# Stick-breaking and differential attention units alternate, and adaLN's rows run between their projections

## The chip, the cores and the metric

One Trainium2 chip; the kernel runs on one core. The metric is the device time of one execution in microseconds (us). The times of before are three runs; a profiled execution stands beside them.

## What is computed

One layer of a hybrid encoder on 1024 prompt rows and 64 sample rows of width 1024, with 1024 cached positions for the sample. All of it is float32; the kernel splits operands into a high and a low part and multiplies three times where it needs float32's precision.

```python
sh1, sc1, ga1, sh2, sc2, ga2 = split(silu(c) @ w_ada + b_ada)   # adaLN
u = (rmsnorm(x) * (1 + sc1) + sh1) @ w_in
# 4 differential heads of 2 x 64: softmax with ALiBi and a chunk mask
a = softmax(s_0) - lam * softmax(s_1);  od = rmsnorm(a @ vd) * (1 - 0.2)
# 8 stick-breaking heads of 64, strictly causal
between = reverse_cumsum(log_sigmoid(-z)) - log_sigmoid(-z)
osb = exp(log_sigmoid(z) + between) @ vs
x = x + ga1 * rmsnorm(concat(od, osb) @ w_out)
x = x + ga2 * rmsnorm(relu(h2 @ w_up)**2 @ w_down)              # h2 from x, sc2, sh2
```

Keys and values of both groups are outputs as well.

## The kernel before

The program has five stages: a setup that loads x and adaLN's first columns, eight attention **units**, the output projection (L1059 to L1062), the feed-forward in 16 blocks, and the end. This case is about the units. Units 0 to 3 are the differential heads, units 4 to 7 are pairs of stick-breaking heads; `unit_cols` (L308) gives the 128 columns of `w_in` that belong to a unit.

A unit consists of three kinds of work:

- **The projection** `proj(u, g)` (L545): q, k and v of the unit for three groups of rows, g = 0, 1, 2 with 384, 384 and 320 rows (`GRP`). Each (u, g) is 72 matmuls in `dense_T` (L303 to L305), 216 for a unit. VectorE (DVE) and ScalarE (ACT) read the result out. After g = 2 of a unit the next unit's weights are loaded and split.
- **Eight steps** over the queries. A differential step `Diff(u, t)` (L635) takes 128 queries: products `pz` (L575, L576), on DVE a minimum with the distance table (L660), on ACT `Exp` (L624), then on DVE the combination of the two softmaxes (L682), transposes on PE (L586), split by ACT and DVE (L64, L65), and the products with V (L602, L603). A stick-breaking step `Stick(u, q, hd)` (L722) takes 256 queries of one head: the products, on ACT two `Sigmoid` (L738, L739), a mask on GpSimd (L720), on DVE a scan along the keys (L712) and a product (L713), then transposes, splits and the products with V (L759, L760).
- **One `Sample(u)`** (L791): the 64 sample rows against the cache, with `Exp` for units 0 to 3 and `Sigmoid` (L867 and the line after it) and scans for units 4 to 7. It stands among the steps of a later unit.

The order is written out by hand. `sections` (L959 to L968) lists the steps unit by unit, 0 to 7, and inserts the samples. The main loop runs the application of one step together with the scores of the next (`merge`, L947) and spends from a `Filler` (L910) meanwhile: a list of projections and of adaLN's remaining rows. `need` (L970) says by which step a projection must be done: group 0 by a unit's first step, group 1 by its third, group 2 by its seventh. So groups 1 and 2 of a unit and group 0 of the next are done during a unit. A scheduler then places the instructions on each engine.

adaLN's **rows** (`rows`: four `gate_rows`, eight pieces of `modulation`; L201, L209, L245) are twelve pieces of filler work. Each loads two blocks of 512 KB of `w_ada` into the three `raw` buffers that the units' weights, the cache and the distance tables use too. Before, two pieces follow the projection's group 2 in each of units 2 to 5, one in unit 6 and three in unit 7 (`others`, L994).

The output projection waits for `mixD`, to which each unit writes its rows, and for their split into `mh` and `ml` (L64, L65).

Of the kernel before, what the change touches and what calls it, by code (L numbers as in the profile page):

```python
# [16 lines left out]
P = 128  # L17
D = 1024
KT = D // P
# [7 lines left out]
GRP = ((0, 384), (384, 384), (768, 320))  # L27
NTT = 9


# [4 lines left out]
def build(tc, I, O):  # L35
    nc = tc.nc
# [274 lines left out]
    def proj_weights(u, i):  # L311
        c = unit_cols(u)[i]
        return weights(w_in[:, :, c : c + P], [P, KT, P], f"w{'qkv'[i]}{u}", el=nc.vector if u == 0 else None)

# [42 lines left out]
    def first(k):  # L357

        for i in range(3):
            drain(dense_T(PS[i], PW[0, i], hT, 0, (k,)))  # L360

    few_columns()
    w0 = [big(f"w{i}0r", "raw", [P, KT, P], F32) for i in range(3)]
    for i in range(3):
        PW[0, i] = big(f"w{i}0h", "w", [P, KT, P]), big(f"w{i}0l", "w", [P, KT, P])

    def first_weights(half, up=False):
        ks = slice(4 * half, 4 * half + 4)
        for i in range(3):
            c = unit_cols(0)[i]  # L370
            if up:
                load(w0[i][:, ks], w_in[:, ks, c : c + P])
                continue
            split(w0[i][:, ks], *(t[:, ks] for t in PW[0, i]), el=nc.vector)

# [97 lines left out]
    def proj_q(u, g, wq):  # L473
# [4 lines left out]
        Q = U[u]["Q"]  # L478
        if u + g:
            ps = bank(f"pq{u}{g}", "pj")  # L480
            yield from dense_T(ps, wq, hT, g)
        else:
            ps = PS[0]
# [10 lines left out]
    def proj_k(u, g, wk):  # L494
# [4 lines left out]
        Kd, Kl = U[u]["Kd"], U[u]["Kl"]  # L499
        if u + g:  # L500
            ps = bank(f"pk{u}{g}", "pj")
            yield from dense_T(ps, wk, hT, g)
        else:
            ps = PS[1]
# [14 lines left out]
    def proj_v(u, g, wv):  # L519
# [3 lines left out]
        V = U[u]["V"]  # L523
        if u + g:
# [20 lines left out]
    def proj(u, g):  # L545
        for i, f in enumerate((proj_q, proj_k, proj_v)):
            if (u, i) not in PW:
                PW[u, i] = proj_weights(u, i)
            for n, c in enumerate(f(u, g, PW[u, i])):
                yield c  # L550

                if u == 0 and g == 1:
                    n += (0, 8, 17)[i]
                    if n >= 5 and (n - 5) % 2 == 0 and (n - 5) // 2 < KT:
                        k = (n - 5) // 2
                        block_mod(block_T(2, k, "tr"), 2, k, nc.gpsimd, k % 2 == 1)
                        yield 0.4
            if g == 2 and u < 7:
                PW[u + 1, i] = proj_weights(u + 1, i)

# [398 lines left out]
    sections = []  # L959
    for u in range(4):  # L960
        sections.append([Diff(u, t) for t in range(8)])
    for u in range(4, 8):
        sections.append([Stick(u, q, hd) for q in range(4) for hd in range(2)])
    for u in range(7):
        if u != 3:
            sections[u + 1].insert((1,1,2,2,1,1,2)[u], Sample(u))
    sections[3].append(Sample(3))
    sections[7].insert(8, Sample(7))  # L968
    steps = [st for sec in sections for st in sec]
    need = []  # L970
    for u in range(8):
        sec = [st for st in sections[u] if not isinstance(st, Sample)]
        for st, g in zip((sec[0], sec[2], sec[6]), range(3)):
            need.append((steps.index(st), (u, g)))
    need.append((len(steps) + 1, "end"))
    cost = [st.cost for st in steps]
    drain(proj(0, 0))
    ready_1()
# [14 lines left out]

    others = {2: (rows, 2, 2), 3: (rows, 2, 2), 4: (rows, 2, 2), 5: (rows, 2, 2), 6: (rows, 1, 1), 7: (rows, 3, 3)}  # L994
    for u in range(8):
        for g in range(3):
            if u + g:
                fill.add(proj(u, g), 12, (u, g))
            if g == (2) and u in others:
                gen, n, c = others[u]  # L1000
                fill.add(some(gen, n), c, "end" if u == 7 else None)
    steps[0].ready()
# [267 lines left out]
```

## Time and profile before

| | us |
|---|---|
| median of three runs | 1586.6 (1586.38 to 1587.48) |
| the profiled execution, its own time | 1589.58 |
| its span | 1587.9 |
| setup (span's start to unit 0) | 54 |
| units 0 to 7 (54 to 694) | 640 |
| output projection (694 to 807) | 113 |
| feed-forward and end (807 to 1588) | 781 |

A unit begins where PE starts its first product `pz`; the boundaries come from the program order of PE laid against the trace. Times in the trace count from the span's start. PE's busy time overlaps itself, since a matmul's end is modelled: how far apart two matmuls start is a better measure of what one costs. In windows of the trace the columns are: the stretch, its length, busy us of PE, PEld (weight load), DVE, ACT and POOL (GpSimd) with the number of instructions in brackets, PE's granted clock as a share of full speed, the share of the DMA engines and GB/s.

### The profile page before, as it was taken

The page shows a single profiled execution, that of the slowest core. Times are in us where ns is not written, and L with a number is a line of the kernel's source. Part 1 is how long each engine was busy: PE and PEld are TensorE (multiplying, and loading weights), DVE is VectorE, ACT ScalarE, POOL GpSimd, SP SyncE. Part 2 cuts the span into 40 slices and gives each one's busy share as a digit, 9 for nine tenths or more (in the row PEclk, how much of TensorE's full clock was granted, in tenths as well). Part 3 has the DMA queues.
Part 4 walks back from the last instruction along what each step waited for, and adds up shares of the span by engine and source line. Part 5 has one row for each costly group of instructions (what it writes and reads, how often), then busy time and mean ns, then how long its engine had stood idle before and what let it go on. Part 6 is the DMA issues. An engine that isn't in the chain of part 4 may idle for free.

```text
span 1587.9 us, 23684 instructions
## 1 busy us (share of the span) xinstructions
PE 1517.0 (96%) x8682; PEld 1357.9 (86%) x8682; DVE 987.2 (62%) x1880; ACT 703.3 (44%) x1665; POOL 366.7 (23%) x580
## 2 busy tenths in 40 slices
PE   6899999999999999789999999999999999999998
PEld 3689988988888889667889888999999899999896
DVE  3777676778789888995552455445544445544447
ACT  3867675766666667656563221121221121221132
POOL 0444352526353434451120000000000000000003
PEclk9999999998999999879999999999999999999999
DMA  9322142432322222364220222021111011111025
GB/s 309 115 60 87 55 116 84 135 95 76 95 74 85 69 70 78 103 208 161 97 63 27 80 80 78 17 79 53 54 42 52 28 41 53 54 41 53 27 80 179
DMA packets 152518, 133.22 MB, mean 84 GB/s; under 512 B 11233, under 2 KB 136274, under 8 KB 152402
## 3 DMA queue, kind: packets, MB, share of 16 engines
q1 hardware_dynamic: 152402, 131.71, 27.2%
q8 instruction: 68, 1.11, 0.3%
q14 instruction: 48, 0.39, 0.1%
HBM read 108.59 MB, written 23.09 MB: 83 GB/s over the span
## 4 chain that ended last, share of the span: by engine, by line
PE 74%; DVE 12%; issue 4%; ACT 3%; DMA 2%; POOL 1%; SPq 0%; POOLq 0%; DVEq 0%; ACTq 0%
PE pu L303 8%; PE pu L304 8%; PE pu L305 8%; PE pd L1145 8%; PE pd L1146 8%; PE pd L1148 7%; DVE k L712 4%; PE py L1059 2%; PE py L1060 2%; PE pt L586 2%; DVE s L713 2%; PE py L1062 2%; PE pq L304 1%; PE pq L303 1%; PE pq L305 1%
## 5 line engine op out<-in xcount | busy, mean ns | idle before, releaser
L1152 DVE TENSOR_TENSOR acc<-pd,acc 128x512 f32<-128x512 f32 x252 | 171.9, 687 | 113.3 <-PE pd L1148 107.2
L1130 ACT ACTIVATE sq<-pu 128x384 f32<-128x384 f32 (+1 forms) x96 | 45.2, 471 | 310.8 <-PE pu L305 310.8
L1131 DVE TENSOR_TENSOR sq<-sq 128x384 f32<-128x384 f32 (+1 forms) x96 | 72.1, 751 | 174.7 <-ACT sq L1130 174.7
L65 DVE TENSOR_TENSOR al<-pt,ah 128x512 fp32r<-128x512 f32 (+2 forms) x128 | 75.5, 599 | 25.7 <-ACT ah L64 24.9
L575 PE MATMUL pz<-K,Q 128*128 128x512 f32 (+2 forms) x192 | 74.8, 393 | 6.4 <-ACT k L739 2.2
L64 ACT CAST ah<-pt 128x512 fp32r<-128x512 f32 (+2 forms) x128 | 65.4, 523 | 33.6 <-PE pt L586 23.2
L586 PE MATMUL pt<-ident,s 128*128 128x128 f32 x432 | 73.7, 288 | 3.3 <-DVE s L713 2.6
L624 ACT ACTIVATE s<-s,mn 128x512 f32<-128x512 f32 (+3 forms) x96 | 58.5, 611 | 26.7 <-DVE mn L660 25.4
L576 PE MATMUL pz<-Kl,qz 128*128 128x512 f32 (+2 forms) x192 | 69.8, 369 | 0.0
L712 DVE TENSOR_TENSOR_SCAN k<-k 128x127 f32<-128x127 f32 (+3 forms) x64 | 62.1, 980 | 4.3 <-POOL k L720 4.0
L713 DVE TENSOR_TENSOR s<-s,k 128x383 f32<-128x383 f32 (+3 forms) x96 | 62.9, 662 | 1.4
L586 PEld LDWEIGHTS pt<-ident,s 128*128 128x128 f32 x432 | 53.1, 147 | 7.6 <-DVE s L713 3.3
L65 DVE TENSOR_TENSOR rl<-sq,rh 128x384 fp32r<-128x384 f32 x64 | 35.7, 558 | 37.9 <-ACT rh L64 37.9
L738 ACT ACTIVATE s<-pz 128x512 f32<-128x512 f32 (+2 forms) x96 | 48.1, 501 | 16.5 <-PE pz L576 12.0
L575 PEld LDWEIGHTS pz<-K,Q 128*128 128x128 f32 x192 | 38.3, 200 | 15.1 <-ACT k L739 4.5
L64 ACT CAST rh<-sq 128x384 fp32r<-128x384 f32 x64 | 32.9, 514 | 40.2 <-DVE sq L1131 38.2
L739 ACT ACTIVATE k<-pz 128x512 f32<-128x512 f32 (+2 forms) x96 | 48.4, 504 | 4.9 <-DVE k L712 4.0
L442 POOL CAST qz<-Q 64x256 fp32r<-64x256 f32 x64 | 34.7, 542 | 66.3 <-PE pz L576 63.9
L760 PE MATMUL po<-al,V 128*128 128x256 f32 (+1 forms) x160 | 43.5, 306 | 6.7 <-DVE al L65 6.6
L759 PE MATMUL po<-ah,V 128*128 128x256 f32 (+1 forms) x160 | 44.9, 292 | 0.5 <-ACT ah L64 0.5
L720 POOL TENSOR_SCALAR_AFFINE_SELECT s<-s 128x128 f32<-128x128 f32 x64 | 30.1, 470 | 63.6 <-ACT s L738 62.9
L660 DVE CUSTOM_DVE_ANT_0 s<-pz,T 128x512 f32<-128x512 f32 (+3 forms) x64 | 37.2, 585 | 10.8 <-PE pz L576 10.3
(1227 smaller groups left out, 5211.3 us busy)
## 6 DMA issues: line engine op xcount, KB each, us to landing
arr<-in_w_ada SPq DMA_DIRECT2D x16, 512.0 KB
arm<-in_w_ada SPq DMA_DIRECT2D x16, 512.0 KB
ar<-in_w_ada SPq DMA_DIRECT2D x10, 512.0 KB
mixD<-mx SPq DMA_DIRECT2D x32, 128.0 KB
xr<-in_x_prompt SPq DMA_DIRECT2D x16, 256.0 KB
xD<-xr SPq DMA_DIRECT2D x16, 256.0 KB
xy<-xD SPq DMA_DIRECT2D x8, 512.0 KB
out_y_prompt<-xy SPq DMA_DIRECT2D x16, 256.0 KB
```

Source lines behind the costliest of these rows:

```text
L64: (eh or nc.scalar.copy)(hi, src)
L65: (el or nc.vector).tensor_tensor(lo, src, fr(hi), ALU.subtract)
L303: mm(ps[:, :n], lhsT=wh[:, k, :], rhs=hh[:, k, :n], start=(k == 0), stop=False)
L304: mm(ps[:, :n], lhsT=wh[:, k, :], rhs=hl[:, k, :n], start=False, stop=False)
L305: mm(ps[:, :n], lhsT=wl[:, k, :], rhs=hh[:, k, :n], start=False, stop=(k == 7))
L575: mm(ps[:, :w], lhsT=S["Q"][m][:, qt], rhs=S["Kd"][m][:, c0 : c0 + w], start=True, stop=False)
L586: nc.tensor.transpose(pt[:kr, i * P : (i + 1) * P], a, ident)
L712: nc.vector.tensor_tensor_scan(k, k, k, 1.0 if c == n - 1 else kp[c + 1][:, 0:1], ALU.mult, ALU.bypass)
L1145: mm(ps, lhsT=rh[:, off : off + P], rhs=wh[:, cols], start=(j == 0), stop=False)
L1146: mm(ps, lhsT=rh[:, off : off + P], rhs=wl[:, cols], start=False, stop=(m == 8 and end))
L1148: mm(ps, lhsT=rl[:, off : off + P], rhs=wh[:, cols], start=False, stop=end)
L1152: nc.vector.tensor_tensor(acc[m][:, cols], ps, acc[m][:, cols], ALU.add)
```

## The change

The units run in the order 4, 0, 5, 1, 6, 2, 7, 3. The sample of each unit stands after the second step of the unit behind it, the last one's before its own last step. The twelve pieces of rows follow groups 0 and 1 of the projections of the third to the eighth unit in the order, one each. Everything that was bound to unit 0 as the first (the weights that the setup prepares, the projection that it finishes, the modulation of the last rows inside it) goes to unit 4.

```diff
+ORDER = (4, 0, 5, 1, 6, 2, 7, 3)
+FIRST = ORDER[0]
...
-            if g == 2 and u < 7:
-                PW[u + 1, i] = proj_weights(u + 1, i)
+            if g == 2 and u != ORDER[-1]:
+                nu = ORDER[ORDER.index(u) + 1]
+                PW[nu, i] = proj_weights(nu, i)
...
-    for u in range(4):
-        sections.append([Diff(u, t) for t in range(8)])
-    for u in range(4, 8):
-        sections.append([Stick(u, q, hd) for q in range(4) for hd in range(2)])
-    for u in range(7):
-        if u != 3:
-            sections[u + 1].insert((1,1,2,2,1,1,2)[u], Sample(u))
-    sections[3].append(Sample(3))
-    sections[7].insert(8, Sample(7))
+    for i, u in enumerate(ORDER):
+        sections.append([Diff(u, t) for t in range(8)] if u < 4 else [Stick(u, q, hd) for q in range(4) for hd in range(2)])
+        if i:
+            sections[i].insert(2, Sample(ORDER[i - 1]))
+    sections[7].insert(8, Sample(ORDER[7]))
...
-    need.append((len(steps) + 1, "end"))
...
-    others = {2: (rows, 2, 2), 3: (rows, 2, 2), 4: (rows, 2, 2), 5: (rows, 2, 2), 6: (rows, 1, 1), 7: (rows, 3, 3)}
-    for u in range(8):
+    for i, u in enumerate(ORDER):
         for g in range(3):
-            if u + g:
+            if i + g:
                 fill.add(proj(u, g), 12, (u, g))
-            if g == (2) and u in others:
-                gen, n, c = others[u]
-                fill.add(some(gen, n), c, "end" if u == 7 else None)
+            if i > 1 and g < 2:
+                fill.add(some(rows, 1), 1)
```

The program order shows what this does on the engines. First ACT, at the sample of unit 0 (`ss0`, `sst0`: its scores; `ah`, `o1`, `mx`: other work of the steps). Before, it stands in unit 1, among that unit's own `Exp` (`s1_...`):

```order
L87 ACTIVATE o10_7_1677,ssd0_7_1680<-od0_7_1676 128x128
L624 ACTIVATE ss0_0_1755,sl0_1823<-ss0_0_1755,smn0_1758 128x512
L624 ACTIVATE ss0_1_1756,sl0_1823<-ss0_1_1756,smn0_1758 128x512
L624 ACTIVATE sst0_1757,sl0_1823<-sst0_1757,smn0_1758 128x64
L530 COPY vf11_1874<-pv11_1782 128x384
L690 COPY o11_0_1792<-po1_0_1690 128x128
L624 ACTIVATE s1_10_0_1845,l1_10_1863<-s1_10_0_1845,mn1_10_1846 128x256
```

After, it stands in unit 5 (lines are three or four higher in the changed file):

```order
L67 CAST ah5_010_2880<-pt5_010_2876 128x384
L628 ACT_TABLE_LOAD
L628 ACTIVATE ss0_0_2957,sl0_3025<-ss0_0_2957,smn0_2960 128x512
L628 ACTIVATE ss0_1_2958,sl0_3025<-ss0_1_2958,smn0_2960 128x512
L628 ACTIVATE sst0_2959,sl0_3025<-sst0_2959,smn0_2960 128x64
L635 ACTIVATE mx0_6_2814<-pm0_6_2815,gsub_113 128x128
L90 ACTIVATE o10_7_2805,ssd0_7_2808<-od0_7_2804 128x128
L742 ACT_TABLE_LOAD
L742 ACTIVATE s5_102_0_3044<-pz5_1020_3046 128x384
```

The three `Exp` of the sample now stand between `Sigmoid` of unit 5, with a table load ahead of them and one behind. Over the whole program ACT has 25 table loads in place of 4.

Second DVE, shortly before the output projection's first operands. Before, these are the scans of the sample and of the last steps of unit 7 (`sk7`, `skt7`, `k7_...`), behind the last projection:

```order
L712 SCALAR_TENSOR_TENSOR skt7_8959<-skt7_8959 128x64
L713 TENSOR_TENSOR sst7_8956<-sst7_8956,skt7_8959 128x63
L712 SCALAR_TENSOR_TENSOR sk7_1_8958<-sk7_1_8958,skt7_8959 128x512
L65 TENSOR_TENSOR al7_300_8898<-pt7_300_8892,ah7_300_8897 128x512
L65 TENSOR_TENSOR al7_301_8924<-pt7_301_8918,ah7_301_8923 128x512
L713 TENSOR_TENSOR ss7_1_8955<-ss7_1_8955,sk7_1_8958 128x511
L712 SCALAR_TENSOR_TENSOR sk7_0_8957<-sk7_0_8957,sk7_1_8958 128x511
L712 SCALAR_TENSOR_TENSOR k7_316_1_9054<-k7_316_1_9054 128x384
L713 TENSOR_TENSOR ss7_0_8954<-ss7_0_8954,sk7_0_8957 128x511
```

After, at the same place, it is the minima of unit 3's last step (`s3_7...`, with `mn3` as their second output) and splits:

```order
L68 TENSOR_TENSOR al3_60_8944<-pt3_60_8938,ah3_60_8943 128x512
L695 TENSOR_TENSOR od3_5_8922<-po3_5_8856,o13_5_8923 128x128
L664 ISA s3_70_1_9070,mn3_70_9071<-pz3_701_9085,T3_8147,mn3_70_9071 128x512
L664 ISA mn3_70_9071 128x1
L68 TENSOR_TENSOR al3_61_8970<-pt3_61_8965,ah3_61_8969 128x384
L664 ISA s3_71_0_9101,mn3_71_9103<-pz3_710_9104,T3_8147 128x512
L664 ISA mn3_71_9103 128x1
L664 ISA s3_71_1_9102,mn3_71_9103<-pz3_711_9114,T3_8147,mn3_71_9103 128x512
```

No scan stands there any more: unit 7's have moved ahead of unit 3's steps.

## Rows read from the trace of the kernel before

**Rows 1.** Busy time in each unit's stretch, output projection and feed-forward (stretch, us, engines, clock, DMA):

```profile
54.00:129.00 75.00, 68.74 (x410) 61.27 (x411) 54.21 (x150) 51.61 (x143) 37.06 (x52) 0.98 0.15 44
129.00:202.00 73.00, 73.00 (x476) 70.30 (x475) 50.34 (x150) 48.04 (x141) 28.76 (x47) 1.00 0.25 74
202.00:279.00 77.00, 72.89 (x462) 63.75 (x460) 54.01 (x154) 49.13 (x146) 30.06 (x50) 0.91 0.35 101
279.00:366.00 87.00, 84.16 (x574) 77.61 (x573) 63.63 (x185) 59.17 (x174) 35.01 (x57) 1.00 0.42 121
366.00:436.00 70.00, 65.64 (x432) 60.00 (x432) 57.07 (x102) 46.59 (x115) 35.00 (x59) 0.93 0.26 78
436.00:520.00 84.00, 78.71 (x532) 73.90 (x531) 74.53 (x122) 54.12 (x127) 34.88 (x59) 0.96 0.27 80
520.00:601.00 81.00, 75.09 (x483) 71.03 (x482) 72.24 (x111) 51.39 (x120) 30.46 (x56) 0.94 0.23 67
601.00:694.00 93.00, 78.69 (x490) 67.99 (x489) 85.07 (x141) 62.43 (x145) 46.94 (x71) 0.85 0.37 109
694.00:807.00 113.00, 109.82 (x513) 89.47 (x513) 68.57 (x119) 66.58 (x157) 24.96 (x52) 0.99 0.43 142
807.00:1588.00 781.00, 773.68 (x4059) 697.13 (x4057) 383.93 (x594) 186.71 (x336) 54.35 (x49) 1.00 0.19 59
```

**Rows 2.** The same view of the end of the last unit:

```profile
630.00:694.00 64.00, 50.03 (x289) 40.00 (x289) 60.64 (x95) 40.98 (x91) 34.37 (x45) 0.78 0.37 116
```

**Rows 3.** Groups of DVE instructions in that stretch (count | busy, mean ns | idle):

```profile
L712 DVE TENSOR_TENSOR_SCAN k<-k 128x511 f32<-128x511 f32 (+5 forms) x11 | 12.4, 1134 | 0.0
L713 DVE TENSOR_TENSOR s<-s,k 128x511 f32<-128x511 f32 (+3 forms) x18 | 12.3, 688 | 0.2
L712 DVE TENSOR_TENSOR_SCAN k<-k,k 128x511 f32<-128x511 f32 x7 | 10.4, 1485 | 0.0
```

**Rows 4.** Waits of PE in the last unit (total us, times, longest us):

```profile
PE po L760 <- DVE al L65: 6.6, 7, 2.0
PE pnk L459 <- DVE mx L779: 2.6, 1, 2.6
```

**Rows 5.** Waits of PE in unit 2:

```profile
PE par L201 <- DMA arr<-in_w_ada: 1.8, 2, 1.6
```

**Rows 6.** Timeline of PE, two matmuls of 384 columns (start us, us):

```profile
180.46 0.34 PE L304 MATMUL pv<-h1l,wv2h 128*128 128x384 f32 x1
180.63 0.34 PE L305 MATMUL pv<-h1h,wv2l 128*128 128x384 f32 x1
```

**Rows 7.** Timeline of ACT where unit 3 ends and unit 4 begins:

```profile
367.54 0.19 ACT L624 ACTIVATION_READ_ACCUMULATOR sst<-sst,smn 128x1 f32 x1
367.74 1.28 ACT L738 ACT_TABLE_LOAD   x1
369.03 0.28 ACT L738 ACTIVATE s<-pz 128x128 f32<-128x128 f32 x1
```

**Rows 8.** Timeline of PE at the same time:

```profile
367.56 0.33 PE L602 MATMUL po<-V,ah 128*128 128x256 f32 x1
367.73 0.23 PE L603 MATMUL po<-V,al 128*128 128x128 f32 x1
367.79 0.51 PE L459 MATMUL pnk<-ident,kf 128*128 128x128 f32 x3
368.06 0.36 PE L575 MATMUL pz<-K,Q 128*128 128x256 f32 x1
368.38 0.31 PE L303 MATMUL pq<-h1h,wq4h 128*128 128x320 f32 x1
368.52 0.31 PE L304 MATMUL pq<-h1l,wq4h 128*128 128x320 f32 x1
```

**Rows 9.** Waits of DVE in unit 5:

```profile
DVE al L65 <- ACT ah L64: 5.1, 3, 3.3
```

**Rows 10.** Groups of DVE instructions over the whole span:

```profile
L660 DVE CUSTOM_DVE_ANT_0 s<-pz,T 128x512 f32<-128x512 f32 (+3 forms) x64 | 37.2, 585 | 10.8 <-PE pz L576 10.3
L682 DVE SCALAR_TENSOR_TENSOR s<-s,cf,s 128x512 f32<-128x512 f32 (+3 forms) x48 | 32.1, 691 | 0.8
L65 DVE TENSOR_TENSOR al<-pt,ah 128x512 fp32r<-128x512 f32 (+2 forms) x128 | 75.5, 599 | 25.7 <-ACT ah L64 24.9
```

More of the change, by code (lines that the diff above doesn't have):

```diff
@@ L312, in proj_weights @@
         c = unit_cols(u)[i]
-        return weights(w_in[:, :, c : c + P], [P, KT, P], f"w{'qkv'[i]}{u}", el=nc.vector if u == 0 else None)
+        return weights(w_in[:, :, c : c + P], [P, KT, P], f"w{'qkv'[i]}{u}")
     PW = {}
@@ L359, in first @@
         for i in range(3):
-            drain(dense_T(PS[i], PW[0, i], hT, 0, (k,)))
+            drain(dense_T(PS[i], PW[FIRST, i], hT, 0, (k,)))
     few_columns()
@@ L364, in build @@
     for i in range(3):
-        PW[0, i] = big(f"w{i}0h", "w", [P, KT, P]), big(f"w{i}0l", "w", [P, KT, P])
+        PW[FIRST, i] = big(f"w{i}0h", "w", [P, KT, P]), big(f"w{i}0l", "w", [P, KT, P])
     def first_weights(half, up=False):
@@ L369, in first_weights @@
         for i in range(3):
-            c = unit_cols(0)[i]
+            c = unit_cols(FIRST)[i]
             if up:
@@ L373, in first_weights @@
                 continue
-            split(w0[i][:, ks], *(t[:, ks] for t in PW[0, i]), el=nc.vector)
+            split(w0[i][:, ks], *(t[:, ks] for t in PW[FIRST, i]), el=nc.vector)
     for q in range(4):
@@ L478, in proj_q @@
         Q = U[u]["Q"]
-        if u + g:
+        if (u, g) != (FIRST, 0):
             ps = bank(f"pq{u}{g}", "pj")
@@ L499, in proj_k @@
         Kd, Kl = U[u]["Kd"], U[u]["Kl"]
-        if u + g:
+        if (u, g) != (FIRST, 0):
             ps = bank(f"pk{u}{g}", "pj")
@@ L523, in proj_v @@
         V = U[u]["V"]
-        if u + g:
+        if (u, g) != (FIRST, 0):
             ps = bank(f"pv{u}{g}", "pj")
@@ L550, in proj @@
                 yield c
-                if u == 0 and g == 1:
+                if u == FIRST and g == 1:
                     n += (0, 8, 17)[i]
@@ L959, in build @@
     sections = []
-    for u in range(4):
-        sections.append([Diff(u, t) for t in range(8)])
-    for u in range(4, 8):
-        sections.append([Stick(u, q, hd) for q in range(4) for hd in range(2)])
-    for u in range(7):
-        if u != 3:
-            sections[u + 1].insert((1,1,2,2,1,1,2)[u], Sample(u))
-    sections[3].append(Sample(3))
-    sections[7].insert(8, Sample(7))
+    for i, u in enumerate(ORDER):
[3 more added lines that the diff above has]
+    sections[7].insert(8, Sample(ORDER[7]))
     steps = [st for sec in sections for st in sec]
     need = []
-    for u in range(8):
-        sec = [st for st in sections[u] if not isinstance(st, Sample)]
+    for u, sec in zip(ORDER, sections):
+        sec = [st for st in sec if not isinstance(st, Sample)]
         for st, g in zip((sec[0], sec[2], sec[6]), range(3)):
             need.append((steps.index(st), (u, g)))
-    need.append((len(steps) + 1, "end"))
     cost = [st.cost for st in steps]
-    drain(proj(0, 0))
+    drain(proj(FIRST, 0))
     ready_1()
@@ L992, in some @@
                 yield c
-    others = {2: (rows, 2, 2), 3: (rows, 2, 2), 4: (rows, 2, 2), 5: (rows, 2, 2), 6: (rows, 1, 1), 7: (rows, 3, 3)}
-    for u in range(8):
+    for i, u in enumerate(ORDER):
         for g in range(3):
-            if u + g:
+            if i + g:
                 fill.add(proj(u, g), 12, (u, g))
-            if g == (2) and u in others:
-                gen, n, c = others[u]
-                fill.add(some(gen, n), c, "end" if u == 7 else None)
+            if i > 1 and g < 2:
+                fill.add(some(rows, 1), 1)
     steps[0].ready()
```

## The prediction

> **What bounds the kernel now.** I read busy time by stage first. The feed-forward takes 781 us of which PE is busy 774, and the output projection 113 with 110 [rows 1]; the change touches neither, so I leave them as they are. What can move is the 640 us of the eight units. There the rows tell two regimes apart. In unit 1 PE is busy for the whole 73 us and DVE for 50: PE is the bound. In units 5 and 6 DVE is busy 74.5 of 84 and 72 of 81, and PE 79 and 75: both are close to full. In unit 7 DVE has 85 of 93, and PE's granted clock falls to 0.85 [rows 1].
>
> The last 64 us of unit 7 are the extreme: DVE 60.6 of 64, PE 50, clock 0.78 [rows 2]. These follow the last projection: no filler is left for PE, and what remains is unit 7's long steps and two stick-breaking samples. The three groups of scans and products shown there make up 35 us of DVE [rows 3], and PE's longest waits in the unit are for DVE (6.6 us for `al`, 2.6 us for `mx`) [rows 4]. Differential units have spare DVE time that is never next to these scans, since they are all done by then.
>
> **Building blocks.** Two matmuls of 384 columns start 0.17 us apart [rows 6], of 320 columns 0.14 us [rows 8]. A unit's projection, 144 of the one and 72 of the other, is 144 x 0.17 + 72 x 0.14 = 34.6 us of PE, or 0.16 us a matmul. A transpose costs 0.09 us (three in 0.27), and a step's value products 0.17 + 0.06 us a block [rows 8]. A stick-breaking unit has 36 more transposes than a differential one (3.2 us) and slightly more value products (about 1): 4 us more PE. On DVE, unit 5 less unit 1 is 74.5 - 50.3 = 24 us [rows 1], of which about 4 are two pieces of rows and the dearer sample: 20 us more DVE.
>
> **The change part by part**, window by window. A window runs from a unit's first product to the next one's. The counts of projection matmuls in it are from the program order: before 232, 269, 172, 263, 172, 221, 214 and 113; after (units 4, 0, 5, 1, 6, 2, 7, 3) 240, 222, 231, 210, 219, 207, 183 and 144.
>
> *First window, unit 4 in place of unit 0.* Before it took 75 us, with PE at 69 and DVE at 54 [rows 1]; it has no sample, and the rest of the modulation stands in it. A stick-breaking unit adds 4 us of PE, 8 more matmuls 1, and DVE gets 20 less some 8 for the last step, whose scans and splits come after the next unit's first product. DVE then has 66 and PE 74 in profile terms: PE still ends last. 75 + 5 = **80 us**, bounds 76 (the stalls of the setup hide the extra) and 86 (DVE's 11 added in full).
>
> *Differential windows 0, 1 and 2.* Unit 1 was 73 us with 269 projection matmuls [rows 1]; now there are 213 on average, 56 x 0.16 = 9 us less PE. Two pieces of rows and the previous unit's last value products add about 3: PE needs 67. DVE had 50 and gets the previous unit's last step and its sample: the order shows three or four scans in each of these windows that were in stick-breaking windows before. With rows that is 50 + 10 = 60. No window of before has this pair, 67 and 60. Unit 1 (PE alone) would give 67; unit 2, which took 77 at a clock of 0.91 and where PE waited for the loads of rows [rows 1, 5], is the other end. I take **72 us** each, nearer the middle, since two pieces of rows are in here as they were in unit 2 but are now apart.
>
> *Stick-breaking windows 5, 6 and 7.* Units 5 and 6 of before are the rows to go by: 84 us with 221 matmuls, 81 with 214 [rows 1]. Now there are 231, 219 and 183. The scans per window are 24, 24 and 22 instead of 27 and 26: the sample in them is a differential one. So 1 to 3 us less DVE, 1 to 2 more PE for the first two, and 31 x 0.16 = 5 less for the third: 84 + 81 + 76 = **241 us**, bounds 226 (each 5 us less, as in unit 4, which had 70 without a sample) and 250.
>
> *Last window, unit 3 in place of unit 7.* This is the largest term. Up to the last projection matmul PE has 144 of them (23 us), most of unit 7's sample and half of unit 3's steps, 42 us in all, with DVE below that; unit 7 took 35 us for its 113. I take 46. Behind it, DVE had 60 us. Now the order shows there, up to the output projection's first operand: eight minima at 0.59 us, four combinations at 0.69 and seven splits at 0.60 [rows 10], some 12 us, and about 6 of short operations: 18 us, and no scan. PE has 18 us there as well (145 instructions, against 245 before). Two engines with 18 us each that feed each other take between 18 and 36; 24 is nearest to what the windows of units 5 and 6 show for such a pair. 46 + 24 = **70 us** where 93 stood, bounds 61 and 85.
>
> *Table loads on ACT.* Every switch between `Exp` and `Sigmoid` costs ACT a load. Before, one stood in the units, 1.28 us, with the next activation starting as it ended [rows 7]; PE went on without a gap meanwhile [rows 8]. Now there are 21 more: 27 us of ACT. ACT has 54 of 84 and 51 of 81 us in the fullest windows [rows 1], so three loads (3.9 us) in a window fit. But they stand in ACT's queue ahead of the casts that transposes need, and DVE and then PE wait behind these. Bounds: 0, as the row shows, and all of 27. The row that is there says 0; since the other places are tighter, I take 0.4 us each, **8 us**.
>
> The Trainium skill (ScalarE: Activation LUTs, Table sets: the hidden batching unit) speaks against the change here: it says to group activations by table set and do all of one set before switching. Its section What ACT_TABLE_LOAD costs states 1283 ns for a load, which the row agrees with, and 2.66 us for a switch with the drain around it, which the row does not show: 0.2 us lie between the starts of the readout before and the load. By its price 21 switches would be 56 us of ACT, and the sum would turn into a loss if they lay on the path.
>
> *Edits at nothing.* Samples are moved, not added; the loads of rows number the same, and the queue SP issues the same transfers. Six of the twelve pieces stand in differential windows, where a distance table holds one of three `raw` buffers, against four before. Unit 2's two waits for them were 1.8 us [rows 5]; two more pieces cost as much, inside the 72. The last `mixD` rows of unit 3 come through a longer end (root on GpSimd, transpose, copy), but the output projection needs them for its seventh block of rows only, some 60 us later. If PE's queue had to wait for that transpose, it would be 2 to 3 us.
>
> **Sum.** 80 + 3 x 72 + 241 + 70 + 8 = 615 us where 640 stood: 25 us less. The profiled execution took 1589.6 us, 3.0 above the median of the runs. 1589.6 - 25 = 1564.6, and against the median 1586.6 - 25 = **1562 us**. The bounds of the terms (5, 15, 12, 12, and 8 down or 19 up for the loads) combine to about 25 either way if they are independent.
>
> **Rivals.**
>
> *The table loads put ACT on the path: slower.* If each of the 21 switches delays the chain by its load and by as much again because casts queue behind it, that is 2.6 us each, 54 us. For it speaks that DVE already waited 5.1 us on ACT's casts in unit 5, once for 3.3 [rows 9]; against it, PE's silence in rows 8. Without the loads the gain is 33, so this rival decides from 1.6 us a switch. The time would be 1586.6 - 33 + 54 = 1608. By the Trainium skill's 2.66 us a switch (same page) it would be 1610.
>
> *The scans only change place: no difference.* The DVE work of the units stays the same in total. If the stick-breaking windows stay at 84 each, the first becomes like unit 7 without samples (90), and the differential ones rise to unit 2's 77, then 90 + 3 x 77 + 3 x 81 + 72 + 4 = 640. For it: DVE in units 5 and 6 is near its limit. Against it: the end is the worst place and loses its scans by the order. Time 1587, from 1580 to 1594.
>
> *DVE's spare time is used fully: a larger gain.* If the differential windows run PE-bound like unit 1 (67), the stick-breaking ones at 226 for three, the first at 76 and the last at 64 with no loads showing: 76 + 201 + 226 + 64 = 567, 73 less, 1514. Half of that is more plausible, 1535 to 1540.
>
> **How the numbers follow.** My forecast (a gain of 8 to 42) gets 0.62, the larger gain 0.12, no difference 0.12 and the slower rival 0.14. Faster and slower count from 0.2%, 3 us, about what a measurement of this kernel can tell from no change. Faster: 0.62 + 0.12 + 0.04 of the third = 0.78; same 0.05; slower 0.14 + 0.03 = 0.17. For eight in ten the range leaves out most of the slower rival and the far part of the larger gain: 1540 to 1592.
>
> **What would show it.** Right: the stretch after the last projection shrinks from 58 to about 24 us with DVE no longer at 95%, the last unit takes 65 to 75, the differential windows lose their full PE but stay near 72, and the clock is back near 1 at the end. ACT shows 25 table loads of 1.28 us with PE's waits for ACT still small. Wrong: stick-breaking windows over 85, the first window at 90 or more, PE waits for `ah` (L64) or DVE waits for `ah` behind table loads of tens of us in sum, or a new wait of PE for `arr` and `arm` in differential windows. The weakest step is the pair of PE 67 and DVE 60 in the differential windows, for which no row stands.

## The result, and the profile after

The changed kernel takes 1601.8 us (median of four runs, 1599.11 to 1603.69) against 1586.5 beside it: ratio 1.010, interval 1.0082 to 1.0119. It is 15 us slower where 25 us less were forecast. Its profiled execution took 1603.69 us with a span of 1602.0.

Busy time by unit of the changed kernel, in the order 4, 0, 5, 1, 6, 2, 7, 3, then output projection and feed-forward (columns as in [rows 1]):

```profile
56.00:139.00 83.00, 75.11 (x446) 67.75 (x447) 75.58 (x120) 59.78 (x135) 44.51 (x70) 0.96 0.14 40
139.00:213.00 74.00, 71.03 (x467) 65.83 (x466) 59.18 (x150) 51.24 (x138) 21.73 (x38) 0.98 0.27 76
213.00:298.00 85.00, 80.93 (x537) 73.23 (x535) 71.88 (x128) 59.63 (x143) 38.79 (x70) 0.98 0.32 94
298.00:375.00 77.00, 73.11 (x487) 65.12 (x486) 57.53 (x154) 52.34 (x140) 24.38 (x41) 1.00 0.31 90
375.00:458.00 83.00, 79.31 (x516) 72.08 (x515) 69.01 (x124) 57.55 (x139) 35.85 (x67) 0.96 0.31 91
458.00:536.00 78.00, 73.92 (x486) 66.52 (x485) 57.63 (x151) 51.67 (x139) 23.77 (x40) 0.98 0.29 87
536.00:610.00 74.00, 68.08 (x466) 61.12 (x464) 62.24 (x113) 54.72 (x133) 37.83 (x63) 1.00 0.35 101
610.00:703.00 93.00, 79.61 (x465) 70.23 (x464) 65.58 (x178) 59.68 (x163) 34.85 (x50) 0.85 0.32 91
703.00:822.00 119.00, 112.52 (x506) 90.76 (x506) 67.33 (x116) 68.65 (x165) 31.56 (x62) 0.96 0.42 138
822.00:1602.00 780.00, 772.79 (x4055) 696.08 (x4053) 383.28 (x592) 185.93 (x333) 54.36 (x49) 1.00 0.19 59
```

To a tenth, the windows are 82.8, 74.0, 85.2, 77.2, 82.5, 78.4, 73.7 and 93.3 us. The last unit is as long as unit 7 was, and its clock is again 0.85, though DVE now has 66 us there and not 85 [rows 1]. The output projection takes 118.6 us instead of 113.3. The feed-forward is unchanged.

The last unit in pieces (same columns):

```profile
610.00:620.00 10.00, 8.35 (x29) 7.54 (x28) 9.65 (x17) 4.05 (x8) 2.88 (x6) 0.51 0.06 20
620.00:630.00 10.00, 10.00 (x70) 10.00 (x70) 4.94 (x12) 4.22 (x10) 0.01 (x1) 0.97 0.01 2
...
640.00:650.00 10.00, 5.74 (x36) 3.58 (x37) 6.22 (x15) 5.44 (x14) 4.98 (x11) 0.72 0.85 225
650.00:660.00 10.00, 10.00 (x55) 9.77 (x55) 4.51 (x12) 4.63 (x14) 2.52 (x5) 0.77 0.14 40
...
670.00:703.00 33.00, 25.52 (x142) 20.45 (x141) 26.69 (x82) 26.86 (x80) 20.80 (x24) 0.90 0.44 138
```

The part behind the last projection matmul, 62.3 us before, shrank to 33.5, and DVE has 26.7 of 33 there instead of 60.6 of 64 [rows 2]. But the part ahead of it grew from 30.8 to 59.8. Most is lost in two stretches of it. At 610 DVE is full (9.65 of 10): the last scans of unit 7 now stand here, and PE's granted clock is 0.51. At 640 PE has 5.7 of 10, and the clock is 0.72 there and 0.77 behind it.

PE's longest waits in this unit (they answer [rows 4]; total us, times, longest us):

```profile
PE pam L204 <- DMA arm<-in_w_ada: 3.2, 1, 3.2
PE pz L579 <- DVE mn L664: 2.4, 2, 1.9
```

And in the output projection:

```profile
PE pm L634 <- POOL od L697: 3.2, 1, 3.2
PE po L607 <- DVE al L68: 2.4, 1, 2.4
```

The wait for `pam` is one for a load of adaLN's rows, and the waits for `mn`, `od` and `al` belong to the steps of the differential unit. The two in the output projection are its last step: its transpose and its value products stand in PE's queue among the output projection's matmuls, and PE waits for their operands there.

### The profile page after: what moved, and what is told of

Its sections match the earlier page's. It is cut to its first block, busy times and chain, and to the rows that moved or that the text cites. A ratio compares the mean times of both kernels' runs of the same rounds, so it can differ in the third digit from the quotient of the medians.

```text
span 1602.0 us, 23684 instructions
## 1 busy us (share of the span) xinstructions
PE 1524.2 (95%) x8682; PEld 1355.2 (85%) x8682; DVE 993.2 (62%) x1880; ACT 729.0 (46%) x1686; POOL 357.4 (22%) x580
## 4 chain that ended last, share of the span: by engine, by line
PE 52%; issue 2%; DVE 1%; POOL 1%; ACT 1%; DMA 0%; SPq 0%; DVEq 0%; POOLq 0%; ACTq 0%
PE pu L306 8%; PE pu L308 8%; PE pu L307 8%; PE pd L1142 8%; PE pd L1143 8%; PE pd L1145 7%; PE py L1057 2%; PE py L1056 2%; PE py L1059 2%; PE ptb L166 0%; DMA mst<-mixD 0%; DVE ml L68 0%; PE par L204 0%; DVE xy L1181 0%; ACT pd L1169 0%
## 5 line engine op out<-in xcount | busy, mean ns | idle before, releaser
L579 PE MATMUL pz<-K,Q 128*128 128x512 f32 (+2 forms) x192 | 72.5, 379 | 10.3 <-DVE mn L664 6.0
L68 DVE TENSOR_TENSOR al<-pt,ah 128x512 fp32r<-128x512 f32 (+3 forms) x128 | 74.7, 598 | 10.6 <-ACT ah L67 9.8
L67 ACT CAST ah<-pt 128x512 fp32r<-128x512 f32 (+3 forms) x128 | 64.3, 522 | 32.1 <-PE pt L590 27.2
L717 DVE TENSOR_TENSOR s<-s,k 128x127 f32<-128x127 f32 (+3 forms) x96 | 69.6, 730 | 1.9
L716 DVE TENSOR_TENSOR_SCAN k<-k 128x127 f32<-128x127 f32 (+3 forms) x64 | 58.4, 914 | 9.0 <-POOL k L724 8.5
L67 ACT CAST r<-sq 128x320 fp32r<-128x320 f32 x32 | 14.8, 462 | 62.7 <-DVE sq L1128 62.7
```

Of the source, the lines that this page charges most:

```text
L67: (eh or nc.scalar.copy)(hi, src)
L68: (el or nc.vector).tensor_tensor(lo, src, fr(hi), ALU.subtract)
L579: mm(ps[:, :w], lhsT=S["Q"][m][:, qt], rhs=S["Kd"][m][:, c0 : c0 + w], start=True, stop=False)
```

## Where the time went

To compare whole kernels I charge each PE instruction in the units and the output projection with the median distance to the next start behind one of its line and shape in the trace of before, 0.17 us for [rows 6]. The same instructions run in every order, so this work is 646 us in all of them. The rest is **loss**: PE waited, or ran at half clock.

| us | before | changed |
|---|---|---|
| setup | 54.3 | 55.9 |
| first seven units: work / loss | 477.6 / 69.3 | 479.3 / 74.5 |
| last unit: work / loss | 62.1 / 31.1 | 61.7 / 31.6 |
| output projection: work / loss | 106.5 / 6.8 | 105.0 / 13.6 |

The loss went from 107.2 to 119.7. The last unit kept its 31 us; the output projection got 7 more, the first seven units 5, the setup 1.6. That is the 14 us between the spans. The setup lies between 53.5 and 56.6 us in all twenty kernels, with no link to the order, so its 1.6 is spread.

## The experiments

Times are medians; before was 1585.7 to 1586.9 beside them. Lengths and losses (in brackets) come from each kernel's profiled execution, one of several: executions of before went from 1579.3 to 1595.05 us in all, so a difference of one or two us between two lengths says little.

| kernel | us | ratio, 95% | first seven | last unit | output proj. |
|---|---|---|---|---|---|
| before | 1586.5 | | 546.8 (69) | 93.1 (31) | 113.3 (7) |
| changed | 1601.8 | 1.0082-1.0119 | 553.8 (75) | 93.3 (32) | 118.6 (14) |
| e1 no switch | 1593.1 | 1.0028-1.0063 | 549.2 (70) | 92.8 (31) | 119.0 (14) |
| e2 old order | 1578.6 | 0.9940-0.9973 | 534.4 (55) | 96.1 (37) | 111.6 (4) |
| e3 sticks first | 1590.9 | 1.0004-1.0042 | 555.1 (71) | 74.8 (22) | 126.2 (18) |
| e4 stick last | 1594.7 | 1.0035-1.0074 | 551.4 (71) | 96.0 (38) | 111.3 (4) |
| e5 rows only | 1591.8 | 1.0024-1.0054 | 533.8 (59) | 109.9 (45) | 110.7 (4) |
| e6 own kind | 1586.8 | 0.9995-1.0014 | 556.4 (70) | 73.7 (22) | 121.1 (14) |
| e7 rows earlier | 1585.8 | 0.9986-1.0006 | 555.7 (67) | 72.5 (22) | 122.5 (16) |
| e8 late finish | 1602.5 | 1.0082-1.0124 | 553.1 (74) | 92.9 (31) | 117.4 (12) |
| e9 both | 1599.1 | 1.0069-1.0116 | 569.3 (69) | 60.1 (25) | 132.1 (21) |
| e10 old order, rows earlier | 1602.6 | 1.0071-1.0127 | 560.5 (76) | 95.8 (42) | 110.4 (3) |
| e11 samples only | 1601.9 | 1.0083-1.0124 | 557.4 (76) | 95.3 (38) | 111.6 (4) |
| e12 diff last | 1586.2 | 0.9986-1.0020 | 555.1 (66) | 72.3 (22) | 120.2 (14) |
| e13 one buffer | 1606.7 | 1.0109-1.0166 | 556.3 (77) | 92.1 (32) | 122.7 (17) |
| e14 sample earlier | 1601.3 | 1.0078-1.0120 | 561.2 (82) | 85.5 (25) | 117.0 (10) |
| e15 sample later | 1593.5 | 1.0025-1.0061 | 560.7 (75) | 81.4 (26) | 115.9 (11) |
| e16 old order, one buffer | 1584.6 | 0.9984-1.0015 | 541.5 (62) | 95.5 (37) | 111.3 (4) |
| e17 before, less DVE | 1557.8 | 0.9804-0.9849 | 531.8 (50) | 77.2 (19) | 111.3 (6) |
| e18 changed, less DVE | 1583.9 | 0.9975-1.0001 | 546.8 (62) | 79.5 (25) | 122.8 (16) |

**Table loads.** e1 replaces the softmax's function in the changed kernel, so ACT loads 4 tables and not 25.

```diff
-            nc.scalar.activation(a, a, AF.Exp, bias=mn, scale=-1.0, accum_out=l[:, i : i + 1])
+            nc.scalar.activation(a, a, AF.Sigmoid, bias=mn, scale=-1.0, accum_out=l[:, i : i + 1])
```

> The changed kernel with the Exp of the differential steps and samples replaced by Sigmoid (the same instruction count and shapes, another function; the differential heads' output is another one), so that ACT needs 4 table loads in place of 25. Theory A (the 21 switches are on the path and are what the change lost): 1575 to 1585 us, 17 to 27 less than the changed kernel's 1602, with the PE waits of the differential windows back to 2 to 6 us. Theory B (the loads hide in ACT's idle time, and the loss is at the end of the last unit): 1597 to 1602, with the last unit still at 90 to 93.

Measured 1593.1, between both: 21 switches cost 8.7 us, 0.4 each (an estimate from both intervals is 5 to 13 us in all). They explain the 5 us of the first seven units (loss 75 to 70), not the rest. The profiled execution of e1 is its slowest (1598.36), so its lengths show less of the gain than the medians.

**Order of the units alone.** One line of the changed kernel, three times:

```diff
-ORDER = (4, 0, 5, 1, 6, 2, 7, 3)
+ORDER = (0, 1, 2, 3, 4, 5, 6, 7)   # e2
+ORDER = (4, 5, 6, 7, 0, 1, 2, 3)   # e3
+ORDER = (0, 4, 1, 5, 2, 6, 3, 7)   # e4
```

> The changed kernel with the units in the old order 0 to 7: what is left of the change is the place of the samples (second step of the next unit) and of adaLN's rows (one after groups 0 and 1 from the third unit on). Theory A and B both: near before, 1583 to 1592, since neither the switches nor a differential end are there. Theory C (the samples' and rows' places cost the time): 1596 to 1604.

> Units in the order 4, 5, 6, 7, 0, 1, 2, 3: differential last, but not in turns, 7 table loads in all. Theory A: it loses only the switches' price against the changed kernel, and keeps the differential end: 1575 to 1588. Theory B: the end of unit 3 is as slow as in the changed kernel (last unit and output projection 205 to 212 us together): 1597 to 1606.

> Units in turns with a stick-breaking one last: 0, 4, 1, 5, 2, 6, 3, 7, with 24 table loads. Theory A: the switches cost as in the changed kernel, and the end is the old one: 1600 to 1612. Theory B: the old end (206 us for the last unit and the output projection) is not slower than the new one (212), so 1590 to 1597.

e2 is below all its ranges and 7 us faster than before: with these places of samples and rows, it is the new order that costs, 23 us. e3 and e4 take its two halves apart. With a differential unit last and no turns (e3) the last unit has 22 us of loss for 37 in e2, but the output projection 18 for 4. With turns and a stick-breaking unit last (e4) it is 38 and 4. With these places neither half gains; e3 falls between its two ranges, e4 is in B's.

**Places alone, in the kernel before.** e5 has only the rows of the change, e11 only the samples:

```diff
+            if u > 1 and g < 2:                      # e5, in place of others
+                fill.add(some(rows, 1), 1)
...
-            sections[u + 1].insert((1,1,2,2,1,1,2)[u], Sample(u))
-    sections[3].append(Sample(3))
+        sections[u + 1].insert(2, Sample(u))         # e11, every u
```

> The kernel before with one part of the change alone: adaLN's twelve rows follow groups 0 and 1 of the projections from the third unit on; order and samples stay. Theory R (the rows' places are what made the old order with the new places 7 us faster than before): 1577 to 1582, with unit 2 back from 77 to about 68 us and no low clock in it. Theory S (the samples' places did it): 1584 to 1589.

> The kernel before with nothing changed but the samples' places: each after the second step of the next unit (unit 3's then stands in unit 4 instead of at the end of its own; table loads 4 to 6). The new places of samples and rows together gave 1578.6 in the old order, and the rows alone 1591.8. If the two add up (theory S), the samples alone give 1572 to 1575. If the rows' new places are good only with the samples' new places (theory P), 1579 to 1587.

Alone they cost 5 and 16 us, outside all four ranges; together (e2) they gain 7. So these edits don't add up, and that in an order where nothing takes turns.

**Rows and samples in the changed kernel.** e7 puts the rows earlier, with none in the last unit. e6 puts each sample two units later, into a unit of its own kind. e9 does both. e10 is e2 with the rows of e7; e12 moves one unit only, with the rows of e7.

```diff
-            if i > 1 and g < 2:
+            if 0 < i < 7 and g < 2:                  # e7, e9, e10, e12
...
-            sections[i].insert(2, Sample(ORDER[i - 1]))
+        if i > 1:                                    # e6, e9
+            sections[i].insert(2, Sample(ORDER[i - 2]))
+    sections[6].append(Sample(ORDER[6]))
...
+ORDER = (0, 1, 2, 4, 5, 6, 7, 3)                     # e12
```

> The changed kernel with each sample in the next unit of its own kind (two units later; unit 7's at its own end), 13 table loads in place of 25. Theory D (the differential windows wait because of the stick-breaking samples in them, the stick-breaking ones because of the Exp in them): 1583 to 1592, the waits of PE in windows 0, 1 and 2 down from 7 to 11 us each to 3 to 6. Theory E (they wait for the last steps of the stick-breaking unit ahead, which stay): 1594 to 1601, of which 5 us are the 12 switches saved at 0.4 us each.

> The changed kernel with the rows after the projections of the second to the seventh unit, none in the last. In the changed kernel PE waited 3.2 us for a load of rows in the last unit, and its clock was at half for some 13 us around it. If that load is what makes the last unit's first part 60 us where 46 was forecast: that part 48 to 52, and 1590 to 1595 in all. If the low clock comes from the step ahead of it: part over 56 and 1598 to 1604.

> Both edits in one kernel: a sample's place in its own kind two units later (unit 7's at the end of its own unit), and the rows' pieces a unit and a half earlier, none in the last unit. Each alone took 15 to 16 us off the changed kernel (1586.8 and 1585.8 against 1602). Theory M, two separate causes (samples of the other kind in the differential units; rows in the last unit): the gains add up, 1571 us (1566 to 1576). Theory N, one cause, the last unit, which each edit alone already brought from 93 to 73 us by taking either the late cache load or the late rows out of it: 1582 to 1589, with a last unit of 62 to 74 us and the rest longer by as much as it gets shorter.

> Units in the old order 0 to 7 with the new samples' places, and the rows' pieces a unit earlier, none in the last unit; with rows as in the change it took 1578.6 us. Theory L, rows in the last unit cost some 16 us whatever the unit: 1562 to 1570. Theory K, they cost only where PE has to do its part of the last unit with nothing else queued, a differential unit with a blocked load queue; in the old order the last unit stands at DVE and the rows there fill PE for nothing: 1576 to 1584.

> One unit moved: order 0, 1, 2, 4, 5, 6, 7, 3, so a differential unit is last but nothing takes turns; samples and rows as in the kernel with 1585.8 us (rows earlier, none in the last unit). Theory T, taking turns costs what the end gains: 1565 to 1575. Theory U, PE's waits in the first seven units come to the same sum, about 67 to 75 us, in whatever order they run: 1580 to 1588, at most 6 us less for fewer table loads.

e6 and e7 each gain 15 to 16 us; e6 is in D's range, e7 better than either of its two. Their last unit takes 73 us, 20 less: 10 of these are loss, the other 10 are work that now stands earlier. The first seven units lose 5 us less in e6, which has 12 table loads less (some 5 us at e1's price), and 8 less in e7, whose output projection gives 2 back. Together they gain 3: the last unit falls to 60, but the work put earlier makes the first seven 14 longer than in e6 or e7, and the output projection takes 132. Theory M falls; of N it holds that the rest grows by nearly what the last unit loses, but the last unit (60) and the time (1599) lie outside its ranges. The same edit of the rows that gains 16 in the new order loses 24 in the old one (e10): K was nearer than L, but both missed. e12 takes no turns and is as fast as e7, which has three times its table loads (27 against 9), so U holds: with these places, taking turns as such costs nothing that shows. A differential unit last does gain with them: e12 and e7 are 16 and 17 us faster than e10, the old order with the same places, whereas with the change's own places e3 is 12 and the changed kernel 23 us slower than e2. What an order is worth depends on the places.

Last unit and output projection of e12 (columns as above):

```profile
612.00:684.00 72.00, 60.82 (x379) 52.20 (x378) 63.02 (x168) 56.30 (x155) 31.89 (x48) 0.95 0.33 103
684.00:804.00 120.00, 112.70 (x517) 91.37 (x518) 68.29 (x117) 69.11 (x166) 36.87 (x63) 0.96 0.42 137
```

The forecast's 70 us for this unit can be had. But then 11 us of PE's work stand earlier, and the output projection is 7 us longer than before.

**Later end.** In the program, e8 finishes the two last steps only where the output projection needs them:

```diff
-            prev.finish()
+            late.append(prev)        # the last two; finished ahead of the last group of rows
```

> The changed kernel with the finish of the last two steps (the transpose and the store of their rows) written behind the output projection's operands of groups 0 and 1. If PE's queue waits there for these transposes (3.4 us for the last, with the clock falling): output projection 112 to 115 us where it is 119, and 1594 to 1598. If the late loads of its weights and operands set the end: 117 to 120, and 1600 to 1604.

Measured 1602.5, in the range of 1600 to 1604, but neither theory is tested by it. The edit moved the transposes in the program and not on the engine: in the trace PE starts the same 8682 matmuls in the same order as in the changed kernel, and its two waits in the output projection are the same in e8:

```profile
PE pm L634 <- POOL od L697: 3.2, 1, 3.2
PE po L607 <- DVE al L68: 2.4, 1, 2.4
```

So e8 is the changed kernel once more, with every window within 1.3 us of it. What these two waits cost stays open.

**The queue of loads.** The queue of SP (SyncE), which issues loads and stores one after the other, in the changed kernel's last unit (start, us, queue, line, transfer):

```profile
613.85 0.37 SPq L810 DMA_DIRECT2D kn<-smD  x1
633.50 0.48 SPq L812 DMA_DIRECT2D vn<-smV  x1
635.50 0.39 SPq L468 DMA_DIRECT2D out_diff_k_prompt<-ok  x1
635.99 0.43 SPq L200 DMA_DIRECT2D arm<-in_w_ada  x1
...
640.08 0.38 SPq L200 DMA_DIRECT2D arm<-in_w_ada  x1
```

Nothing was issued for 20 us: the sample's load `vn` stood at the head, and the rows' loads behind it. It waited for a buffer, until DVE had split `kn`:

```profile
SPq L812 <- DVE bd L68: 17.7, 1, 17.7
```

e13 gives `kn` and `vn` one buffer; e16 does it in e2.

```diff
-            kn = small([P, 2, TS], f"kn{u}", "kf")
-            vn = small([TS, P], f"vn{u}", "kf")
+            kv = small([P, 4, TS], f"kv{u}", "kf")
+            kn, vn = kv[:, 0:2, :], kv[0:TS, 2:4, :].rearrange("p a b -> p (a b)")
```

> The changed kernel, with the sample's two small loads from smD and smV in one buffer, so that the second no longer waits until DVE has split the first (17.7 us in the last unit, with the rows' loads queued behind it). Theory Q, that block of the queue makes the last unit 93 us instead of about 75: last unit 74 to 84 us, time 1584 to 1594. Theory R, the rows' loads come late for another reason as well, or the last unit's loss (waits and half clock, 31 us) is in the chains between DVE, ACT and PE: last unit 90 to 96, time 1597 to 1604.

> The fastest kernel so far (old order of units, new places of samples and rows, 1578.6 us) with the sample's two small loads in one buffer. Theory Q: no block of the queue to remove near the end, so 1576 to 1581, or a few us less where smaller blocks delay a sample. Theory V (any move of a load changes which chains meet): outside 1574 to 1583.

The same place in e13, and what its queue waited for:

```profile
614.08 0.37 SPq L811 DMA_DIRECT2D kv<-smD  x1
614.50 0.47 SPq L812 DMA_DIRECT2D kv<-smV  x1
635.99 0.39 SPq L468 DMA_DIRECT2D out_diff_k_prompt<-ok  x1
636.48 0.43 SPq L200 DMA_DIRECT2D arm<-in_w_ada  x1
```

```profile
SPq L468 <- DVE ok L467: 26.2, 2, 20.9
```

The wait was removed, and the next in line took its place: the store of the projection's keys waited 20.9 us for its readout, and the rows' load left 0.5 us later than before the edit. Q falls. R's last unit holds (92.1), and its time is 3 us above R's range. Whether the loads of rows would help if they left at 614 is not shown: they stand behind that store too.

**One step.** e14 and e15 put each sample one step earlier or later:

```diff
-            sections[i].insert(2, Sample(ORDER[i - 1]))
+            sections[i].insert(1, Sample(ORDER[i - 1]))   # e14
+            sections[i].insert(3, Sample(ORDER[i - 1]))   # e15
```

> The changed kernel with each sample after the first step of the next unit instead of the second; nothing else. Theory V, the sum of PE's waits depends on which chains happen to meet, so that such a shift alone moves the time by 5 us or more either way: below 1597 or above 1607. Theory W, the alternation itself costs the 15 us: 1598 to 1606.

> The changed kernel with each sample after the third step of the next unit instead of the second; nothing else. Theory V (the sum of PE's waits depends on which chains meet): below 1597 or above 1607. Theory W (the alternation itself costs the 15 us): 1598 to 1606.

e14 changes nothing in sum (its last unit gains 8 us and the others lose as much), e15 gains 8. e16, the same buffer edit in the old order, lost 6. So theory V is right in one of the two steps and in e16: one step of the samples' place is worth up to 8 us.

**DVE's load.** e17 takes the scans' product from before, e18 from the changed kernel, and both leave a part of the stick-breaking weights out. These are 108 instructions in either, 72 us of DVE in before (the first expectation has 106 and 68) and 83 in the changed kernel:

```diff
-            nc.vector.tensor_tensor(s[c][:, : w - 1], s[c][:, : w - 1], kp[c][:, 1:w], ALU.mult)
```

> The kernel before without DVE's product of the sticks' scans (`s` times `k`, 94 in the steps and 12 in the samples, 68 us of DVE), so the stick-breaking heads weight by the sigmoid alone; the scans stay. Theory D, DVE's load bounds the stick-breaking units and the end: the last unit falls by 12 us or more, the units 4 to 6 by 4 to 8 each, 1550 to 1566. Theory C, the chains of the steps bound: only the link of 0.7 us falls out of some chains, the last unit by 3 to 8, the sum by 5 to 18: 1568 to 1582.

> The changed kernel without the same products (stick-breaking heads weighted by the sigmoid alone, 83 us of DVE). Theory D, DVE's load bounds where scans stand, and the change had moved them to where DVE has room: less to gain here than in the kernel before, 1585 to 1597, and the distance to e17 grows to 25 us or more. Theory C, the chains bound in either order: about the same gain in both, 1582 to 1597, distance 10 to 20 us.

Before gains 28 us, the changed kernel 18; the distance grows from 15 to 26. For before, D's time and last unit hold; of units 4 to 6 only one fell by the 4 us it asked for. e18 is 1 us below D's range and inside C's, at D's distance. So DVE's load bounds a part of the kernel before, as was thought, and it seems to matter less in the new order; but the difference of 10 us is little more than the 8 that one step of the samples' place is worth, so this second part is not firm. Unit 7 of e17, and the last unit of e18 in its first 30 us:

```profile
586.00:663.00 77.00, 65.41 (x467) 57.85 (x466) 68.19 (x105) 60.08 (x142) 42.43 (x68) 0.93 0.42 132
```

```profile
603.00:613.00 10.00, 10.00 (x71) 10.00 (x71) 7.37 (x20) 5.83 (x15) 1.06 (x3) 1.00 0.01 2
613.00:623.00 10.00, 10.00 (x73) 8.57 (x73) 6.51 (x18) 9.20 (x26) 2.55 (x2) 1.00 0.49 129
623.00:633.00 10.00, 6.47 (x32) 4.46 (x33) 5.46 (x13) 5.13 (x15) 5.48 (x13) 0.71 0.75 215
```

In e17 unit 7 fell from 93.1 to 77.2, units 4, 5 and 6 by 3.5, 5.8 and 2.3, and unit 2, which holds none of these products, by 4.6. In e18 the last unit's first 10 us run at full clock, where the changed kernel had 0.51, so without unit 7's last products that stretch is gone. The second one, with the rows' loads, is still there (0.71). But the scans alone don't make the first one either. In e7, which keeps them and has the rows a unit earlier, DVE is as full there, but PE has work and stays at full clock:

```profile
610.00:620.00 10.00, 9.64 (x58) 8.34 (x57) 9.75 (x22) 9.24 (x21) 2.64 (x5) 1.00 0.15 42
```

## Why the prediction was wrong, point by point

- **Table loads: right in number and price.** 25 as counted, 8.7 us for 8 (e1; 5 to 13 by the intervals). The 0.4 us was picked between bounds of 0 and 27 in all, so that it comes this near is luck. DVE's waits for `al`'s operand `ah` fell from 24.9 us [rows 10] to 9.8. The rival with 54 us is excluded.
- **The sum of the eight windows** is 647.1 us for 615. The four window terms made 607 of these, and they are over by 2.8, 13.6, 0.4 and 23.3 us, with the table loads inside them. Output projection and setup, which stood at no change, add 5.3 and 1.6.
- **Stick-breaking windows 5, 6, 7: right, in part by luck.** 85.2 + 82.5 + 73.7 = 241.4 for 241. But the term was without table loads, and e1, which has none there, takes 235.2. First window 82.8 for 80, inside its bounds.
- **Differential windows: mis-sized.** 229.6 for 216. The pair behind it was right: PE's work is 66.8, 68.1 and 67.5 us for the forecast 67, and DVE has 59.2, 57.5 and 57.6 for 60. What failed is the step from the pair to a time, "72, nearer the middle": loss is 7, 9 and 11 us, not 5. Unit 2's 77 was the row to go by. Table loads are not what is missing: in e1 the three come to 228.9. In e18 they come to 216.0, 9 of the 13.6 us because less of PE's work falls into them and 5 because it waits less.
- **The last window: the step that failed most.** 93.3 for 70. Its tail did shrink, to 33.5 for 24. PE's work in it is 18 us, as forecast; I also read unit 7 wrongly, as 35 + 58 us where the trace has 30.8 + 62.3. "Up to the last projection 46" came to 59.8: PE's work there is 43.6 for 42, but I gave it 4 us of loss. It got 16, most of them in the two stretches above: at the last scans of unit 7, which I had counted as gone from the end, and at the wait for the rows' load, which I had priced at 1.8 us inside a differential window ("edits at nothing").
- **The output projection "as it is": wrong.** 118.6 for 113.3. All eleven kernels with a differential unit last (changed, e1, e3, e6 to e9, e12 to e15) have 115.9 to 132.1 here, the seven with a stick-breaking one last (before, e2, e4, e5, e10, e11, e16) 110.4 to 113.3. I had named the place (the transpose behind the root on GpSimd, 2 to 3 us) and left it out of the sum. In the trace the difference is the 3.2 us of `pm` above and 2.4 of `po`, with half clock behind them; no run takes these waits out.
- **The premise.** I took the end's 30 us of loss for a property of the scans. Loss in last unit and output projection together is 38 us before and 35 to 48 in the eleven kernels with a differential unit last. The best of them (e6, e12 and e14) save some 3 us there, not 23. DVE's load was part of it (e17), but a differential step's own chain from `pz` to `mixD` leaves PE waiting as well (for `mn`, `al` and `od`), and does so later.
- **The rivals.** In time the slower one is nearest (1608), but e1 excludes its cause. In mechanism it is "the scans only change place": e6, e7 and e12 stand at 1586 to 1587, its 1587. The changed kernel is another 15 above them. Of these, 10 are loss in its last unit, where rows, sample 7 and the last scans of unit 7 meet; e6 takes the sample away, e7 the rows, and each loses the 10. The other 5 or 6 are in the first seven units: in e6 about the price of its 12 table loads, in e7 not explained.

Not settled: why one placement of rows and samples has 96 us of loss and another 121. In the old order of units six kernels with the same work go from 1578.6 to 1602.6, in the new one eight (e8 among them) from 1585.8 to 1606.7. No single wait explains it: the loss is spread over dozens of waits of 0.5 to 5 us, and removing one (e13) brings up the next. My sum had no term for this spread; every bound in it was a window's own.

The fastest kernel with all the work is e2: the old order of units with the change's places of samples and rows, 0.44% below before (0.27 to 0.60).

## What to carry to other kernels

Moving work of a saturated engine away from the end gains only what no other chain takes up there: write down what the last stage waits for when that work is gone, and charge the stage behind it too. Where an order by hand feeds in-order queues, two edits that gain 15 us each may give 3 together, so measure the pair, and measure a one-step shift to learn how much of a result is placement. Taking work out (e17, e18) tells what an engine's load is worth; moving it doesn't. And look in the trace whether an edit moved what it was meant to move: e8 moved nothing on PE, so its time says nothing about its theory.

## What the runs showed of the hardware

**A table switch cost less than its load here.** ACT in the changed kernel, two groups of the 25 loads over the span (count, busy us, mean ns):

```profile
L628 ACT ACT_TABLE_LOAD x11 | 14.1, 1283 | 1.3 <-DVE mn L664 1.1
L742 ACT ACT_TABLE_LOAD x7 | 9.0, 1283 | 0.1
```

Each takes 1283 ns, but 21 of them moved the time by 8.7 us, 0.4 each; ACT has 51 to 60 of the 74 to 85 us in the first seven windows. The Trainium skill (ScalarE: Activation LUTs, What ACT_TABLE_LOAD costs) states 1283 ns, which the rows agree with; its 2.66 us for a switch would have made 56 us, which e1 does not show.

**A few idle microseconds were followed by ten at half clock.** PE in the changed kernel (start us, us; in brackets the wait ahead of it):

```profile
609.25 0.39 PE L764 MATMUL po<-al,V 128*128 128x256 f32 x1 [1.30 <-DVE al L68]
...
611.31 1.54 PE L590 MATMUL pt<-ident,s 128*128 128x128 f32 x6 [1.20 <-DVE s L717]
...
615.87 0.52 PE L306 MATMUL pq<-h1h,wq3h 128*128 128x384 f32 x1
616.19 0.52 PE L307 MATMUL pq<-h1l,wq3h 128*128 128x384 f32 x1
...
620.79 0.34 PE L307 MATMUL pq<-h1l,wq3h 128*128 128x384 f32 x1
620.96 0.34 PE L308 MATMUL pq<-h1h,wq3l 128*128 128x384 f32 x1
```

Behind these waits the granted clock is 0.51 from 610 to 620, the lower of its two levels (1.2 GHz; the higher is 2.4): matmuls of 384 columns start 0.32 us apart and from 620.6 on 0.17 again [rows 6]. So these waits were charged twice. The wait of 3.2 us for the rows' load has 0.72 and 0.77 around it in the same way, and a forecast of 1.8 us for a load was short by this too.

**A product on DVE waited for a whole GpSimd instruction.** DVE in unit 1 of the changed kernel, then GpSimd at the same time:

```profile
333.61 3.21 DVE L717 TENSOR_TENSOR ss<-ss,sk 128x511 f32<-128x511 f32 x1
...
338.19 0.69 DVE L717 TENSOR_TENSOR ss<-ss,sk 128x511 f32<-128x511 f32 x1
```

```profile
333.73 0.18 POOL L719 TENSOR_TENSOR ss<-ss,sk 128x1 f32<-128x1 f32 x1
333.88 2.40 POOL L68 TENSOR_TENSOR wv6l<-wv6r,wv6h 128x1024 fp32r<-128x1024 f32 x1
```

The same product takes 0.69 us alone and 3.21 where GpSimd's split of a weight (2.40 us) runs beside it. Instructions of DVE that are over 0.5 us longer than the short ones of their shape lose 39 us in the units and the output projection of before, and 48 in the changed kernel. There are 26 of them before and some 30 after; all work from SBUF alone, and beside each a GpSimd instruction runs for over 0.5 us. I had taken DVE's work as the same in any order. The Trainium skill (SBUF — State Buffer, SBUF: two separate sides) says that a DVE instruction with two inputs in SBUF and a GpSimd instruction that reads SBUF share a port pair, which one of them holds for the whole instruction while the other blocks. The rows agree in the time lost; the page gives the pair to the one that starts first, and these starts (333.61 for DVE, 333.88 for GpSimd) don't show that. The sum does not follow the times, though: e2 has 32 us of it and e10 also 32.
